# A decoder block on one core: the stage ahead of the first projection, with x's last tile shared by two engines, two rows of the sums on GpSimd, and modulation row block by row block

## The chip, the core and the metric

The kernel runs on one core of a Trainium2 chip. The engines are named as the profile names them: PE (TensorE, matmuls; PEld is its weight loads), DVE (VectorE), ACT (ScalarE), POOL (GpSimd) and SP (SyncE, which issues nearly all loads and stores). Each engine works through its own queue in order; semaphores join the queues. The metric is device time in microseconds (us) of the whole program.

## The reference, cut to what matters

One layer: a modulated RMSNorm, one input projection whose columns feed a gMLP branch and an attention branch, an output projection, a gated residual and a last RMSNorm. SEQ is 512, D_MODEL 2048, everything float32. The change touches only what comes before the input projection:

```python
cond = jax.nn.silu(c)
mod = cond @ w_ada[l] + b_ada[l]
shift, scale, gate = jnp.split(mod, 3, axis=-1)
h = rms_norm(x, norm_g[l]) * (1.0 + scale[:, None, :]) + shift[:, None, :]
z = h @ w_in[l]
```

`rms_norm` divides each row of x by the root of its mean square (plus 1e-6) and multiplies by `norm_g`. `c` has one row, so `cond @ w_ada` is a product of one vector with a 2048 x 6144 matrix.

## The kernel before

**Tiles.** x is loaded as four tiles `x0` to `x3` of 128 rows (positions) by 2048 columns, 1 MB each. The projection wants h with features on the partitions, so each normalised tile is transposed on PE in blocks of 128 x 128: `xT[kb]` holds feature block kb (0 to 15) for all 512 positions. After modulation each block is split in two, `hh` (rounded to the matmul's type) and `hl` (the rest), and each weight tile in `whi` and `wlo`; a product is hh·whi + hl·whi + hh·wlo, lines L147 to L149.

**Before the first matmul of the projection** these chains run.

1. Norm, lines L305 to L310, a loop over the four x tiles: ACT squares the tile and sums along the row (`ssq`), DVE multiplies by 1/D and adds the epsilon (L90), POOL raises the one column to the power -0.5 (L91), DVE scales the 128 x 2048 tile (L308).
2. Transposes, L318: four of them (one for each x tile) make one PSUM bank `xTp`; ACT copies the bank out to `xT` (L325). Seven banks are in use, so PE is at most seven feature blocks ahead of ACT.
3. The shift and scale of the first two feature blocks, `ada_step(0, i)` and `make_h(0)`. Shift and scale are sums over 16 row blocks ("rows" kk below) of `w_ada`, each row block weighted with a column of `sc`, which is silu(c). Row blocks come in pairs (`ada_i` holds rows 2i and 2i+1, two loads of 256 KB). Most rows are summed on DVE into `accs`, 128 x 512 in SBUF (L244 for row 0, L246 for the others). The rows in `MV = (7, 9, 11, 13, 15)` go to PE instead as matmuls that move a single column, `sc`, and add up in four columns of the PSUM bank `cb` (L239). In `make_h(0)` four matmuls with a column of ones add the 128 partitions of `accs` to the same four columns (L258); DVE forms `sh` and `gs` from them (L263 to L265); ACT makes `hh` (L269); for block 0 DVE makes `h` (L276) and `hl` (L283).
4. The first weight tiles, `raw_st`: ACT rounds them (L131, `whi`), POOL subtracts (L132, `wlo`).

After that the projection runs on PE, in stages of two feature blocks. For the next stage the same sums are made by DVE while PE works, with one difference: there the running sum `acc` lies in PSUM. `make_h(q)` then comes as a few small matmuls (`mod`) in the middle of PE's queue.

**What sets the order.** The kernel is written as a sequence, and a scheduler places each instruction in the queue of its engine by priority (`high_priority`) and by its own estimate of times; `issue_after` pins one instruction behind another. The order is fixed when the program is built. SP's loads are chained in the order of the code, and a load waits for the buffer it writes: the `ada` tiles have eight buffers, so the first pair of the next stage goes into the buffer of `ada_0`, the second into that of `ada_1`, and so on. Each load also waits for the load eight places before it. At the start PE runs 18 bf16 matmuls on a mask (`warm`, L193), whose product is not used.

Of the kernel before, what the change touches and what calls it, by code (L numbers as in the profile page):

```python
# [27 lines left out]
def trunk_kernel(  # L28
# [68 lines left out]
    WARM = 0  # L97

# [79 lines left out]
    rows = st.tile([64, P], F32, name="rows")  # L178
    for r0, nr, src in (
        (16, 32, b_ada[0, 0 : 2 * D]), (0, 16, norm_g[0]), (48, 8, ln_g[0]), (56, 8, ln_b[0]),  # L180
    ):
        nc.scalar.dma_start(rows[r0 : r0 + nr, :], src.rearrange("(a b) -> a b", b=P))
# [8 lines left out]
    def warm(lhs, rhs, n, first=False):  # L191
        for i in range(n):
            nc.tensor.matmul(  # L193
                cb[:, P : P + rhs.shape[-1]], lhs, rhs, start=first, stop=True, skip_group_check=True
            )
# [24 lines left out]
    MV = (7, 9, 11, 13, 15)  # L220

    def ada_step(q, i):
# [3 lines left out]
        for s in range(2):  # L226
            load(ga[:, :, s, :], ada_r[:, 2 * i : 2 * i + 2, s, k0 * P : k0 * P + 256])
        if i == 0:
# [3 lines left out]
        a, sb = accs[q]  # L232
        for j in range(2):
            kk = 2 * i + j
            col = sc[:, kk : kk + 1]
            if q == 0 and kk in MV:
                for s in range(2):
                    for n in range(2):
                        newest_mm[0] = nc.tensor.matmul(  # L239
                            cb[:, 2 * s + n : 2 * s + n + 1], ga[:, j, s, n * P : (n + 1) * P], col,  # L240
                            start=(kk == MV[0] and s + n == 0), stop=False, skip_group_check=True,
                        )
            elif kk == 0:
                nc.vector.tensor_scalar(a, ga[:, j], col, None, ALU.mult)  # L244
            else:
                nc.vector.scalar_tensor_tensor(  # L246
                    sb if kk == KB - 1 else a, ga[:, j], col, a, ALU.mult, ALU.add
                )
# [3 lines left out]

    def make_h(q):
        k0, nk = ADA[q]
        mp = bank("c", f"mod{q}") if q else cb
        for s in range(2):
            for j in range(nk):
                newest_mm[0] = nc.tensor.matmul(  # L258
                    mp[:, s * nk + j : s * nk + j + 1], accs[q][1][:, s, j * P : (j + 1) * P],
                    ones[:, 0:1], start=q > 0, stop=True, skip_group_check=True,  # L260
                )
        ks = slice(k0, k0 + nk)
        nc.vector.tensor_tensor(sh[:, ks], mp[:, 0:nk], bshT[:, ks], ALU.add)  # L263
        nc.vector.tensor_tensor(gs[:, ks], mp[:, nk : 2 * nk], b1[:, ks], ALU.add)
        nc.vector.tensor_tensor(gs[:, ks], gs[:, ks], ngT[:, ks], ALU.mult)  # L265
        for k in range(k0, k0 + nk):
            hh[k] = act.tile([P, S], F32R, tag="hh", name=f"hh{k}")
            hl[k] = act.tile([P, S], F32R, tag="hl", name=f"hl{k}")
            z = nc.scalar.activation(  # L269
                hh[k], xT[k], AF.Identity, bias=sh[:, k : k + 1], scale=gs[:, k : k + 1]  # L270
            )
            h = xT[k]
            if k == 0:
                first_h[0] = z
                h = st.tile([P, S], F32, name="h0", tag="acc", bufs=2)
                nc.vector.tensor_scalar(  # L276
                    h, xT[k], gs[:, k : k + 1], sh[:, k : k + 1], ALU.mult, ALU.add
                )
            else:
                nc.scalar.activation(  # L280
                    xT[k], xT[k], AF.Identity, bias=sh[:, k : k + 1], scale=gs[:, k : k + 1]
                )
            (nc.vector if k == 0 else HL).tensor_tensor(hl[k], h, hh[k].bitcast(F32), ALU.subtract)  # L283
# [18 lines left out]
    ssq = st.tile([P, NT], F32, name="ssq")  # L302
    rstd = st.tile([P, NT], F32, name="rstd")
    for t in range(NT):
# [4 lines left out]
        if t < 3:  # L309
            warm(ident, xt[t][:, 0:P], WARM)  # L310
# [843 lines left out]
```

## Time and profile before

| | us |
|---|---|
| median of 3 runs | 905.56 |
| lowest and highest of them | 905.46 and 912.02 |
| the profiled execution | 903.07 |
| its span, first to last instruction | 901.3 |
| around the span | 1.77 |

The profile is of one execution. Its chain of waits goes back from the last instruction to what released each step. A row of the timeline gives start, duration, engine, line, operation, output and inputs, shape, how many instructions are merged in it, and in brackets how long the engine was idle before it and what ended that. The duration of merged rows runs to the end of the last one. A matmul of float32 with one moving column shows as two records, so `make_h(0)`'s four matmuls are eight. Ends of matmuls are modelled; the distance between starts tells the pace.

### The profile page before, as it was taken

Reading aid. Unit: us, or ns where it says so; the run is one execution under the profiler, and the core shown is the slowest. Engines: PE = TensorE matmul, PEld = TensorE weight load, DVE = VectorE, ACT = ScalarE, POOL = GpSimd, SP = SyncE. Lnnn points to the kernel's source line nnn. Section 1 sums busy time; section 2 is a strip of 40 time slices with the busy share of each in tenths; the row PEclk is TensorE's granted clock in tenths of the full one; section 3 lists DMA queues with packets and bytes.
Section 4 is the critical chain, followed back from the end, with each engine's and each line's share of the span. In section 5 each row is a group of like instructions: output and inputs, shape, how many; then the busy total and the mean of one; then the engine's idle time right before and its main releaser. Section 6 shows DMA issues by size and latency. Waiting matters only on the chain.

```text
span 901.3 us, 12686 instructions
## 1 busy us (share of the span) xinstructions
PE 878.5 (97%) x4408; PEld 744.5 (83%) x4408; DVE 596.3 (66%) x982; ACT 444.6 (49%) x775; POOL 438.1 (49%) x338
## 2 busy tenths in 40 slices
PE   6999999999999999999999999999999999999995
PEld 4988888887888997778789888998898888888884
DVE  4768888374436866455786563456764679997687
ACT  5653332442213224465666554557465657554454
POOL 2355555425676359988998879444751000000001
PEclk7899999999999999999999999999999999999998
DMA  9999996438996164554554545677576246577575
GB/s 339 352 352 356 354 318 212 121 108 292 312 317 201 40 186 124 161 161 133 174 165 140 166 130 187 199 234 221 186 249 188 71 126 209 182 252 248 177 238 203
DMA packets 139712, 188.91 MB, mean 210 GB/s; under 512 B 9968, under 2 KB 103360, under 8 KB 139136
## 3 DMA queue, kind: packets, MB, share of 16 engines
q1 hardware_dynamic: 139216, 187.53, 65.0%
q8 instruction: 35, 0.57, 0.3%
q10 hardware_dynamic: 432, 0.57, 0.2%
q14 instruction: 29, 0.24, 0.1%
HBM read 166.90 MB, written 20.97 MB: 208 GB/s over the span
## 4 chain that ended last, share of the span: by engine, by line
PE 88%; DVE 4%; DMA 3%; issue 2%; ACT 2%; POOL 0%; SPq 0%; POOLq 0%; ACTq 0%; DVEq 0%
PE s L149 6%; PE s L147 6%; PE s L148 6%; PE vb L156 3%; PE vb L157 3%; PE vb L158 3%; PE va L158 3%; PE va L156 3%; PE va L157 3%; PE q L147 3%; PE q L149 3%; PE q L148 3%; PE gb L149 3%; PE k L149 3%; PE gb L148 3%; PE gb L147 3%
## 5 line engine op out<-in xcount | busy, mean ns | idle before, releaser
L608 POOL TENSOR_SCALAR gate<-gate,sc 128x512 f32<-128x512 f32 x60 | 106.4, 1783 | 22.6 <-DMA gate<-in_w_ada_dram 13.6
L132 POOL TENSOR_TENSOR wlo_st<-raw_st,whi_st 128x1024 fp32r<-128x1024 f32 (+3 forms) x36 | 68.4, 1905 | 51.3 <-ACT whi_st L131 48.0
L609 POOL TENSOR_TENSOR gate<-gate,gate 128x512 f32<-128x512 f32 x60 | 91.7, 1530 | 1.8
L148 PE MATMUL s<-hl,whi_st 128*128 128x512 f32 x224 | 86.8, 390 | 0.0
L147 PE MATMUL s<-hh,whi_st 128*128 128x512 f32 x224 | 86.7, 392 | 0.0
L654 POOL TENSOR_TENSOR ts<-ts 128x256 f32<-128x256 f32 x64 | 57.1, 898 | 58.2 <-DMA ts<-in_w_out_dram 55.3
L66 ACT ACTIVATE whi_p<-p 128x1024 fp32r<-128x1024 f32 x52 | 55.2, 1061 | 55.1 <-PE woZ L938 20.1
L67 DVE TENSOR_TENSOR wlo_p<-p,whi_p 128x1024 fp32r<-128x1024 f32 x52 | 63.4, 1221 | 20.2 <-ACT whi_p L66 20.1
L246 DVE SCALAR_TENSOR_TENSOR acc<-ada,sc,acc 128x512 f32<-128x512 f32 x98 | 73.9, 754 | 3.4 <-DMA ada<-in_w_ada_dram 0.5
L149 PE MATMUL s<-hh,wlo_st 128*128 128x512 f32 x224 | 76.2, 392 | 0.0
L157 PE MATMUL vb<-whi_vb,hl 128*128 128x256 f32 (+1 forms) x256 | 72.2, 285 | 0.0
L156 PE MATMUL vb<-whi_vb,hh 128*128 128x256 f32 (+1 forms) x256 | 72.0, 285 | 0.0
L158 PE MATMUL vb<-wlo_vb,hh 128*128 128x256 f32 (+1 forms) x256 | 71.3, 288 | 0.0
L981 POOL TENSOR_TENSOR sfin<-sfin,nhalf 128x1 f32<-128x1 f32 x2 | 1.5, 748 | 137.7 <-DVE sfin L1073 137.7
L131 ACT ACTIVATE whi_st<-raw_st 128x1024 fp32r<-128x1024 f32 (+3 forms) x36 | 31.3, 871 | 65.1 <-PE s L148 38.8
L147 PE MATMUL q<-hh,whi_q 128*128 128x512 f32 x128 | 50.6, 395 | 1.3 <-ACT whi_q L131 1.3
L132 DVE TENSOR_TENSOR wlo_va<-raw_va,whi_va 128x1024 fp32r<-128x1024 f32 x16 | 26.0, 1626 | 38.0 <-ACT whi_va L131 33.9
L147 PE MATMUL k<-hh,whi_k 128*128 128x512 f32 x128 | 50.2, 392 | 0.7 <-ACT whi_k L131 0.7
L147 PE MATMUL gb<-hh,whi_gb 128*128 128x512 f32 x128 | 50.4, 394 | 0.3 <-ACT whi_gb L131 0.3
L156 PE MATMUL va<-whi_va,hh 128*128 128x512 f32 x128 | 50.3, 393 | 0.0
L148 PE MATMUL q<-hl,whi_q 128*128 128x512 f32 x128 | 50.2, 392 | 0.0
L148 PE MATMUL gb<-hl,whi_gb 128*128 128x512 f32 x128 | 50.2, 392 | 0.0
(308 smaller groups left out, 2541.9 us busy)
## 6 DMA issues: line engine op xcount, KB each, us to landing
ada<-in_w_ada_dram SPq DMA_DIRECT2D x128, 256.0 KB
gate<-in_w_ada_dram SPq DMA_DIRECT2D x32, 512.0 KB
p<-ts SPq DMA_DIRECT2D x32, 512.0 KB
p<-in_w_out_dram SPq DMA_DIRECT2D x24, 512.0 KB
raw_va<-in_w_in_dram SPq DMA_DIRECT2D x16, 512.0 KB
raw_q<-in_w_in_dram SPq DMA_DIRECT2D x16, 512.0 KB
raw_k<-in_w_in_dram SPq DMA_DIRECT2D x16, 512.0 KB
raw_gb<-in_w_in_dram SPq DMA_DIRECT2D x16, 512.0 KB
```

The costliest lines, as they stand in the source:

```text
L67: return a, (eng or nc.vector).tensor_tensor(lo, src, hi.bitcast(F32), ALU.subtract)
L132: (loeng or nc.vector).tensor_tensor(lo, raw, hi.bitcast(F32), ALU.subtract)
L147: nc.tensor.matmul(pt, hi[:, j, cs], hh[k], start=(k == first), stop=False)
L148: nc.tensor.matmul(pt, hi[:, j, cs], hl[k], start=False, stop=False)
L149: nc.tensor.matmul(pt, lo[:, j, cs], hh[k], start=False, stop=(k == last))
L156: nc.tensor.matmul(o, ah[k][:, tsl], hi[:, j, :], start=(k == first), stop=False)
L157: nc.tensor.matmul(o, al[k][:, tsl], hi[:, j, :], start=False, stop=False)
L158: nc.tensor.matmul(o, ah[k][:, tsl], lo[:, j, :], start=False, stop=(k == last))
L246: nc.vector.scalar_tensor_tensor(sb if kk == KB - 1 else a, ga[:, j], col, a, ALU.mult, ALU.add)
L608: nc.gpsimd.tensor_scalar(ga[:, j], ga[:, j], sc[:, kk : kk + 1], None, ALU.mult)
L609: nc.gpsimd.tensor_tensor(a, a, ga[:, j], ALU.add)
L654: nc.gpsimd.tensor_tensor(dst, l, r, ALU.subtract)
```

## The change

- **x3.** ACT squares and sums only the first 1024 columns of `x3`; DVE does the other 1024 in one instruction (`tensor_tensor_reduce`, which starts from the epsilon term), then adds ACT's sum and divides by D. POOL's power is as before. DVE scales the first 1024 columns, ACT the other 1024.
- **Table.** A Square of one column is put on ACT between the first of its loads and the others, so ACT's table load comes there.
- **Rows.** `MV` becomes (11, 13, 15): rows 7 and 9 go to DVE. Rows 2 and 3 (`ada_1`) leave DVE: POOL multiplies each with its column of `sc` and adds the two, and DVE adds the result to `accs` in one instruction ahead of row 10. Row 14, the last on DVE, is done as two instructions, one for each feature block.
- **PE's order.** All transposes of blocks 0 to 13 come first (`HB` goes from 12 to 13), then rows 11, 13, 15, with four mask matmuls (`GAPW`) ahead of row 13 and four ahead of row 15.
- **Modulation.** `make_h(0)` takes the two feature blocks one after the other: two matmuls with ones, `sh`, `gs`, `hh` for block 0, then the same for block 1.

The core of the diff:

```diff
-    MV = (7, 9, 11, 13, 15)
+    MV = (11, 13, 15)
...
+        if q == 0 and i == 1:
+            for j in range(2):
+                nc.gpsimd.tensor_scalar(ga[:, j], ga[:, j], sc[:, 2 + j : 3 + j], None, ALU.mult)
+            nc.gpsimd.tensor_tensor(ga[:, 0], ga[:, 0], ga[:, 1], ALU.add)
+            side.append(ga)
+            return
+        if q == 0 and i == 5:
+            nc.vector.tensor_tensor(a, a, side[0][:, 0], ALU.add)
...
+                    if kk > MV[0]:
+                        warm(cmask[:, 0:P], cmask[:, 0 : S - P], GAPW, after=newest_mm[0])
...
-                nc.vector.scalar_tensor_tensor(
-                    sb if kk == KB - 1 else a, ga[:, j], col, a, ALU.mult, ALU.add
-                )
+                for c_ in ((slice(0, P), slice(P, 2 * P)) if q == 0 and kk == KB - 2 else (slice(0, 256),)):
+                    nc.vector.scalar_tensor_tensor(
+                        (sb if kk == KB - 1 else a)[:, :, c_], ga[:, j, :, c_], col, a[:, :, c_],
+                        ALU.mult, ALU.add,
+                    )
...
+            nc.scalar.activation(
+                junk[:, 0:HD], xt[t][:, 0:HD], AF.Square, accum_out=ssq[:, t : t + 1]
+            )
+            rt = rstd[:, t : t + 1]
+            nc.vector.tensor_tensor_reduce(
+                out=junk[:, HD:D], in0=xt[t][:, HD:D], in1=xt[t][:, HD:D], scale=1.0,
+                scalar=EPS * D, op0=ALU.mult, op1=ALU.add, accum_out=rt,
+            )
+            nc.vector.tensor_tensor(rt, rt, ssq[:, t : t + 1], ALU.add)
+            nc.vector.tensor_scalar(rt, rt, 1.0 / D, None, ALU.mult)
+            power = nc.gpsimd.tensor_tensor(rt, rt, nhalf[:, 0:1], ALU.pow)
+            scaled = XS.tensor_scalar(xt[t][:, 0:HD], xt[t][:, 0:HD], rt, None, ALU.mult)
+            nc.scalar.activation(xt[t][:, HD:D], xt[t][:, HD:D], AF.Copy, scale=rt)
...
+                if i < 2:
+                    es.enter_context(tc.issue_after((power if i else scaled).ins))
+                ada_sums(0, i, loaded[i])
-    HB = 12
+    HB = 13
```

In DVE's queue, around the scaling of x3 and the sums, there stood before (x_105 is x3; accs is the running sum; ada_i the pair of rows 2i and 2i+1; lines of the kernel before):

```order
L204 COPY cols<-cols_p 128x64
L212 TENSOR_SCALAR b_137<-cols 128x16
L244 TENSOR_SCALAR accs_145<-ada_0_142,sc 128x512
L90 TENSOR_SCALAR rstd<-ssq 128x1
L246 SCALAR_TENSOR_TENSOR accs_145<-ada_0_142,sc,accs_145 128x512
L308 TENSOR_SCALAR x_105<-x_105,rstd 128x2048
L246 SCALAR_TENSOR_TENSOR accs_145<-ada_1_148,sc,accs_145 128x512 x2
L246 SCALAR_TENSOR_TENSOR accs_145<-ada_2_153,sc,accs_145 128x512 x2
L246 SCALAR_TENSOR_TENSOR accs_145<-ada_3_158,sc,accs_145 128x512
```

In the changed kernel the same queue, from the scaling of x3 (now x_107, half of it) to the first `sh`, reads:

```order
L366 TENSOR_SCALAR x_107<-x_107,rstd 128x1024
L275 TENSOR_SCALAR accs_192<-ada_0_144,sc 128x512
L278 SCALAR_TENSOR_TENSOR accs_192<-ada_0_144,sc,accs_192 128x512
L278 SCALAR_TENSOR_TENSOR accs_192<-ada_2_150,sc,accs_192 128x512 x2
L278 SCALAR_TENSOR_TENSOR accs_192<-ada_3_153,sc,accs_192 128x512 x2
L278 SCALAR_TENSOR_TENSOR accs_192<-ada_4_156,sc,accs_192 128x512 x2
L256 TENSOR_TENSOR accs_192<-accs_192,ada_1_147 128x512
L278 SCALAR_TENSOR_TENSOR accs_192<-ada_5_159,sc,accs_192 128x512
L278 SCALAR_TENSOR_TENSOR accs_192<-ada_6_162,sc,accs_192 128x512
L278 SCALAR_TENSOR_TENSOR accs_192<-ada_7_165,sc,accs_192 128x2x128 x2
L319 TENSOR_TENSOR sh<-cb,cols 128x1
```

Before, two rows were summed ahead of x3's scaling and nine behind it; now all of them stand behind it: eleven rows, the last of them in two halves, and the addition of POOL's result.

POOL's queue of the changed kernel, from the powers to the first weight tile, where three instructions are new (the third and fourth row below):

```order
L91 TENSOR_TENSOR rstd<-rstd,nhalf 128x1 x3
L365 TENSOR_TENSOR rstd<-rstd,nhalf 128x1
L251 TENSOR_SCALAR ada_1_147<-ada_1_147,sc 128x512 x2
L252 TENSOR_TENSOR ada_1_147<-ada_1_147 128x512
L133 TENSOR_TENSOR wlo_st_1_0_0_377<-raw_st_1_0_0_373,whi_st_1_0_0_376 128x512
```

The two multiplications and the addition for rows 2 and 3 stand right behind x3's power, where DVE's half scaling of x3 and its sums also begin.

PE's queue of the changed kernel behind the last transpose of block 13 (cb is the bank of the sums; the first row stands between the mask matmuls, whose weight loads the order lists too):

```order
L267 MATMUL cb<-sc,ada_6_162 128x1 x4
L199 LDWEIGHTS cmask
L199 MATMUL cb<-cmask 128x384
L199 LDWEIGHTS cmask
L199 MATMUL cb<-cmask 128x384
L199 LDWEIGHTS cmask
L199 MATMUL cb<-cmask 128x384
L199 LDWEIGHTS cmask
L199 MATMUL cb<-cmask 128x384
L267 MATMUL cb<-sc,ada_7_165 128x1 x4
L312 MATMUL cb<-ones,accs_192 128x1 x4
L381 MATMUL xTp_348<-ident,x_101 128x128
```

Before, the matmuls with ones were followed by three blocks of transposes (twelve) and then the projection; now by two blocks (eight). Further on the order of every engine is what it was.

More of the change, by code (lines that the diff above doesn't have):

```diff
@@ L97, in trunk_kernel @@
     WARM = 0
+    GAPW = 4
     newest = [None]
@@ L189, in trunk_kernel, with warm @@
     cb = bank("c", "cb")
-    def warm(lhs, rhs, n, first=False):
+    def warm(lhs, rhs, n, first=False, after=None):
         for i in range(n):
-            nc.tensor.matmul(
-                cb[:, P : P + rhs.shape[-1]], lhs, rhs, start=first, stop=True, skip_group_check=True
-            )
+            with ExitStack() as es:
+                if after is not None:
+                    es.enter_context(tc.issue_after(after.ins))
+                nc.tensor.matmul(
+                    cb[:, P : P + rhs.shape[-1]], lhs, rhs, start=first, stop=True,
+                    skip_group_check=True,
+                )
     warm(cmask[:, 0:P], cmask[:, 0 : S - P], BUSY, True)
@@ L236, in ada_step, with moving @@
             if q == 0 and kk in MV:
-                for s in range(2):
+                def moving(ga=ga, j=j, kk=kk, col=col):
+                    if kk > MV[0]:
+                        warm(cmask[:, 0:P], cmask[:, 0 : S - P], GAPW, after=newest_mm[0])
                     for n in range(2):
[L239 to L242, printed above, removed]
+                        for s in range(2):
+                          with tc.issue_after((newest_mm[0] or newest_tr).ins):
+                            newest_mm[0] = nc.tensor.matmul(
+                                cb[:, 2 * s + n : 2 * s + n + 1], ga[:, j, s, n * P : (n + 1) * P],
+                                col, start=(kk == MV[0] and s + n == 0), stop=False,
+                                skip_group_check=True,
+                            )
+                later_mm.append(moving)
             elif kk == 0:
@@ L255, in make_h @@
         mp = bank("c", f"mod{q}") if q else cb
[L256 to L283, printed above, removed]
+        for z in range(nk if q == 0 else 1):
+            js = [z] if q == 0 else list(range(nk))
+            for s in range(2):
+                for j in js:
+                    newest_mm[0] = nc.tensor.matmul(
+                        mp[:, s * nk + j : s * nk + j + 1], accs[q][1][:, s, j * P : (j + 1) * P],
+                        ones[:, 0:1], start=q > 0, stop=True, skip_group_check=True,
+                    )
+            ks = slice(k0 + js[0], k0 + js[-1] + 1)
+            m0 = mp[:, js[0] : js[-1] + 1]
+            m1 = mp[:, nk + js[0] : nk + js[-1] + 1]
+            nc.vector.tensor_tensor(sh[:, ks], m0, bshT[:, ks], ALU.add)
+            nc.vector.tensor_tensor(gs[:, ks], m1, b1[:, ks], ALU.add)
+            nc.vector.tensor_tensor(gs[:, ks], gs[:, ks], ngT[:, ks], ALU.mult)
+            if q == 0:
+                modulate(k0 + z)
@@ L285, in ada_steps @@
+        if q:
+            for k in range(k0, k0 + nk):
+                modulate(k)
     def ada_steps(q):
```

54 lines of the change are left out of this document (44 added, 10 removed).

## The prediction

> **What bounds the kernel now.** I read the page's first lines, then the chain of waits over the first 60 us, then the table of stretches, then the timeline there. From the page:
>
> ```profile
> span 901.3 us, 12686 instructions
> PE 878.5 (97%) x4408; PEld 744.5 (83%) x4408; DVE 596.3 (66%) x982; ACT 444.6 (49%) x775; POOL 438.1 (49%) x338
> ```
>
> PE is busy 97% of the span, so 23 us without PE work are all there is, most of it ahead of the projection. The change can only move the projection's start; behind it PE's queue is unchanged, so a move of the start goes to the end as it is, if nothing later catches it. The chain of waits (start, length, what) there:
>
> ```profile
> 17.31 1.06 POOL rstd L91
> 18.39 1.30 DVE x L308
> 22.34 0.93 PE xTp L318 x8
> 24.94 3.54 PE cb L239 x24
> 28.48 1.71 PE cb L258 x8
> 30.18 2.66 PE xTp L318 x12
> 32.85 1.35 PE s L147 x5
> 47.36 0.79 PE mod L258 x8
> ```
>
> x3's scaling (L308) is the last thing PE waits for; from 19.7 on PE itself is the chain. The same kind of instruction has two paces: a transpose takes 0.93/8 = 0.116 us at 22.3 and 2.66/12 = 0.222 at 30.2; a record with one moving column takes 1.71/8 = 0.214 at 28.5 and 0.79/8 = 0.099 at 47.4. The table of stretches (from:to, length, busy time of PE, PEld, DVE, ACT, POOL with counts, granted clock, DMA share, GB/s) shows why:
>
> ```profile
> 16.09:19.50 3.41, 2.76 (x13) 2.35 (x12) 2.93 (x7) 0.17 (x2) 1.05 (x1) 0.50 1.10 350
> 19.50:22.92 3.42, 3.18 (x30) 3.19 (x31) 3.28 (x6) 2.82 (x6) 0.00 (x0) 1.00 1.10 349
> 22.92:26.33 3.41, 3.41 (x35) 3.41 (x32) 2.83 (x4) 3.41 (x8) 0.00 (x0) 1.00 1.11 353
> 26.33:29.74 3.41, 3.41 (x18) 3.41 (x17) 0.75 (x1) 1.29 (x3) 1.94 (x2) 0.50 1.08 346
> 29.74:33.15 3.41, 3.41 (x17) 3.31 (x17) 2.90 (x8) 2.41 (x5) 0.27 (x1) 0.50 1.10 351
> 33.15:36.56 3.41, 3.41 (x17) 2.80 (x16) 3.27 (x5) 1.90 (x4) 1.30 (x1) 1.00 1.10 353
> ```
>
> The granted clock halves at 26.33, behind a stretch of mostly single-column records, and comes back at 33.15, behind one full of transposes. Before, the projection runs at half clock until 33.15; its start counts as 32.9 at full pace (it begins at about 32.65, as the twelve transposes end, and loses half of 0.5 us).
>
> DVE does not bind before: its sums end at 27.10 and then it waits 3.12 us for PE. These rows carry the terms below:
>
> ```profile
> 14.56 0.55 POOL L91 TENSOR_TENSOR rstd<-rstd,nhalf 128x1 f32<-128x1 f32 x1 [1.46 <-DVE rstd L90]
> 17.31 1.05 POOL L91 TENSOR_TENSOR rstd<-rstd,nhalf 128x1 f32<-128x1 f32 x1 [2.20 <-DVE rstd L90]
> 14.25 1.91 ACT L306 ACTIVATE junk<-x 128x2048 bf16<-128x2048 f32 x1 [0.20 <-DMA x<-in_x_dram]
> 15.14 1.29 DVE L308 TENSOR_SCALAR x<-x,rstd 128x2048 f32<-128x2048 f32 x1 [0.67 <-POOL rstd L91]
> 16.68 0.48 DVE L244 TENSOR_SCALAR accs<-ada,sc 128x512 f32<-128x512 f32 x1
> 17.20 0.75 DVE L246 SCALAR_TENSOR_TENSOR accs<-ada,sc,accs 128x512 f32<-128x512 f32 x1
> 19.60 6.26 DVE L246 SCALAR_TENSOR_TENSOR accs<-ada,sc,accs 128x512 f32<-128x512 f32 x8
> 26.35 0.75 DVE L246 SCALAR_TENSOR_TENSOR accs<-ada,sc,accs 128x512 f32<-128x512 f32 x1 [0.50 <-DMA ada<-in_w_ada_dram]
> 30.22 0.16 DVE L263 TENSOR_TENSOR sh<-cb,cols 128x2 f32<-128x2 f32 x1 [3.12 <-PE cb L258]
> 30.57 0.75 DVE L244 TENSOR_SCALAR acc<-ada,sc 128x512 f32<-128x512 f32 x1
> 30.74 1.52 ACT L269 ACTIVATE hh<-xT,sh,gs 128x512 fp32r<-128x512 f32 x2 [2.60 <-DVE gs L265]
> ```
>
> **The change, part by part.**
>
> *x3 and the table load.* x3 lands at 14.25 (ACT waited for it), and the table load ahead of x0 is no longer the first thing ACT does with x, so only x0 to x2 can be earlier. Four 1 MB tiles arrive evenly, x2 some 2.5 us ahead of x3, at 11.7; its square (1.91) and sum, DVE's small step, POOL's power (0.55) bring DVE to x2's scaling at about 14.7, done at 16.0 (before: 16.43). Only then does DVE's queue reach its half of x3's squares. No such row exists; the custom DVE reduction of 128x512 costs:
>
> ```profile
> L491 DVE CUSTOM_DVE_ANT_0 s<-s,cmask 128x512 f32<-128x512 f32 x16 | 11.4, 714 | 3.0 <-PE s L490 3.0
> ```
>
> so 1024 columns cost 0.7 to 1.4, taken 1.3 (double, less one start), to 17.3. Reading the sum, the copy of `cols` and three small steps, 0.1 to 0.2 each: 17.9. Power 0.55: 18.5. Before, it ended at 18.36. So sharing x3 gives nothing up to the factor. Half the scaling lies between 0.48 (512 columns) and 1.29 (2048), 0.75: 19.25 in place of 19.68, 0.4 us won for PE.
>
> *PE.* 35 transposes are left then (7 + 28), 24 single-column records and eight mask matmuls. By the paces above the first two take 4.1 + 2.4 us all at full clock, 7.8 + 5.1 at half. The mask matmuls:
>
> ```profile
> 1.52 5.21 PE L193 MATMUL cb<-cmask 128*128 128x384 bf16 x18 [1.52 <-POOL cmask L74]
> ```
>
> 0.29 each, 2.3 for eight, half of that were those all at half clock. PE is through at 27.1 (row 15 lands at 26.35, by DVE's wait, and costs 0.8) to 34.5; with the clock back after one busy stretch, as at 19.50, about 30. The 16 records less are worth 1.6 to 3.4 us, but only if PE is still last.
>
> *DVE becomes last.* Behind 18.5 it has the half scaling 0.75, row 0 0.45, seven rows at 6.26/8 = 0.78 (5.5), the addition 0.72, two rows 1.56, and the first half of row 14, between 0.38 and 0.75, 0.45: 9.4 us, to 27.9, the second half to 28.35. Rows 7 and 9, moved from PE, take the place of 2 and 3, and the two that stood ahead of x3's scaling come behind it. That is already 0.8 later than 27.10, and POOL's work is not in it yet.
>
> *Two rows on POOL.* Their price is in the gate stage:
>
> ```profile
> L608 POOL TENSOR_SCALAR gate<-gate,sc x60: 1559/1568/2637, 329.4 to 560.0; 128x512 f32<-128x512 f32 x60
> L609 POOL TENSOR_TENSOR gate<-gate,gate x60: 1275/1292/3976, 331.0 to 562.9; 128x512 f32<-128x512 f32 x60
> ```
>
> 2 x 1.57 + 1.28 = 4.4 us, from 18.5 to 22.9, ahead of DVE's addition at about 25. It looks hidden. But minimum and maximum lie far apart, and a pair of rows shows what stretches them:
>
> ```profile
> 217.43 1.28 POOL L633 TENSOR_TENSOR tsptl<-tsptl 128x512 f32<-128x512 f32 x1
> 217.46 2.33 DVE L132 TENSOR_TENSOR wlo_va<-raw_va,whi_va 128x1024 fp32r<-128x1024 f32 x1 [2.50 <-ACT whi_va L131]
> L67 DVE TENSOR_TENSOR wlo_p<-p,whi_p 128x1024 fp32r<-128x1024 f32 x52 | 63.4, 1221 | 20.2 <-ACT whi_p L66 20.1
> ```
>
> The same DVE form takes 1.22 alone and 2.33 when it starts 0.03 behind a POOL instruction: it waits it out, less 0.14 us of start. POOL waits likewise: x3's power took 1.05, not 0.55, beside row 1 on DVE (17.20 to 17.95). `accs` and `ada` are both in SBUF, as in these pairs. So each of POOL's three instructions stops DVE for its length: 4.4 - 3 x 0.14 = 4.0 us. The bounds are 0 (they fall into DVE's own waits, of which it has none here) and 4.4. I take 4.0: first half at 31.9, second at 32.35.
>
> The Trainium skill, "SBUF — State Buffer", section "Who interferes with whom", says a DVE instruction with two SBUF inputs contends with a GpSimd instruction that reads SBUF, and whichever is first holds the shared pair for its whole instruction. By that the term is the full 4.4 us and the sum 0.4 later.
>
> *Row block by row block.* Block 0 needs two matmuls with ones (four records): 0.86 at half clock. Half clock, because PE waits from about 30 to 31.9 behind single-column records, as at 26.33. Then `sh` and `gs` 0.45, `hh` 0.8: 31.9 + 0.86 + 0.1 + 0.45 + 0.05 + 0.8 = 34.15. PE meanwhile does block 1's four records to 33.65 and eight transposes at 0.213 to 35.35, and starts there. `hl` (h 0.54, three small steps 0.42, `acc` 0.75, `hl` 0.69 behind 33.3) is there at 35.7, before the sixth matmul. The clock is back after a stretch of transposes, at 36.56 if the boundaries stay; 1.2 us at half pace cost 0.6.
>
> *Loads.* The second pair of the next stage goes into `ada_1`'s buffer, now free only after DVE's addition, 18.5 + 0.75 + 0.45 + 5.5 + 0.72 + 4.0 = 29.9; all later loads queue behind it on SP.
>
> ```profile
> 24.82 1.07 SPq L107 DMA_DIRECT2D ada<-in_w_ada_dram  x2
> 43.67 0.75 DVE L246 SCALAR_TENSOR_TENSOR accs<-ada,sc,acc 128x512 f32<-128x512 f32 x1
> ```
>
> They are 5.1 us late. Their sums ended at 44.42 for a consumer at 47.36, 2.9 of slack, and PE is 3 later itself: hidden, barely.
>
> *Sum.* Start at full pace 35.35 + 0.6 = 35.95 against 32.9: +3.05 us, on 903.07 (span 901.3) 906.1. The median of the runs shown, 905.56, is 2.5 above the profiled execution. Clock boundaries need not fall alike in each execution, and a start that waits for DVE depends less on them, so I don't add the 2.5 in full: 906.6.
>
> **Rivals.**
>
> *POOL doesn't stop DVE: faster.* One mechanism: the three instructions run beside the sums. First half at 27.9; with the clock held, ones 0.4, `sh` and `gs` 0.5, `hh` 0.8: 29.6, 0.35 for `hl`, so 29.95 and -2.95, which the 2.9 of slack at 47.36 also allows: 900.2; with the clock lost 902.1. It decides where DVE is held up by less than 4.0 - 3.05 = 1.0 us. For it: the one overlapping row of this very form, at 17.20, was not itself stretched. Against it: there POOL came second, and paid.
>
> *The clock stays up.* The eight mask matmuls are there between the single-column rows. Then ones 0.4, block 0's `hh` at 33.7, the transposes done with it, and `hl` (35.25) holds the sixth matmul up by 0.35: 34.1, +1.2, 904.3. Against it: 22.92 to 26.33 held more transposes than the mask matmuls amount to, and the next stretch was at 0.50.
>
> The skill's "TensorE: Matmul & The Clock Gate", Part 1, has the clock fall after an idle stretch of 3.4 us. PE would hardly be idle so long; by that rule this rival holds, with its 904.3. The row at 22.92 speaks against it: PE listed busy for all 3.41 us, and the next at 0.50.
>
> *One more stretch at half clock, or the late loads show.* 3.4 us at half pace are +1.7: 907.8; PE through only at 34.5 gives 906.1 + 2.6 = 908.7; loads not hidden by PE's own delay, 5.1 - 2.9 more: 908.3.
>
> *No difference:* the terms cancel, within 0.5 of 903.07 to 905.56.
>
> **How the numbers follow.** Forecast 0.50 (905.5 to 907.2); clock stays up 0.13; faster rival 0.22 (900.2 to 902.1 on the profiled execution, up to 904.6 by the runs); slower rivals 0.10; no difference 0.05. Range 902.6 to 909.0: it leaves out the faster rival's lower half and the longest tail. A measurement of this kernel tells a change from none at about 1%, 9 us; no case here moves so far, so within 1% is 0.96, faster 0.01, slower 0.03 (a lot of runs like the 912.02).
>
> **What would show it.** Right: DVE's sums end near 32 with rows of 2 us among them, POOL's L251 rows above 1.57, PE idle before the matmuls with ones, the projection at 35 to 36. Wrong: ten rows at 0.75 beside POOL's (faster rival); granted clock 1.00 from 26 to 36; PE waiting at `mod` near 50 (loads).

## The result, and the profile after

| | before | after |
|---|---|---|
| median of 22 runs each, same chip, us | 904.88 | 911.53 |
| lowest and highest | 902.58, 912.02 | 907.30, 915.78 |
| ratio to before, 95% interval | | 1.0057, 1.0041 to 1.0073 |
| profiled execution, its span | 903.07, 901.3 | 911.00, 908.9 |

The changed kernel is slower by 6.65 us, where 906.6 was predicted (902.6 to 909.0). In a second comparison on another occasion (below) it was 1.0045, 1.0019 to 1.0070, that is 4.8 us. The two profiled executions lie 7.6 us apart.

The page's first lines of the changed kernel say as little as those of before: PE still 97% busy.

```profile
span 908.9 us, 12686 instructions
PE 880.3 (97%) x4400; PEld 744.0 (82%) x4400; DVE 604.7 (67%) x990; ACT 445.6 (49%) x777; POOL 441.0 (49%) x341
```

The table of stretches of the changed kernel, cut at its clock's own boundaries (from:to, length, busy time of PE, PEld, DVE, ACT, POOL, granted clock, DMA share, GB/s):

```profile
21.72:25.13 3.41, 3.41 (x32) 3.30 (x32) 3.30 (x4) 3.41 (x9) 0.65 (x1) 1.00 1.11 347
25.13:28.54 3.41, 2.75 (x24) 2.38 (x21) 3.21 (x5) 2.07 (x5) 1.43 (x1) 1.00 1.09 352
28.54:31.96 3.42, 1.15 (x5) 1.06 (x5) 2.64 (x6) 0.00 (x0) 1.63 (x2) 0.50 1.10 347
31.96:35.37 3.41, 3.41 (x15) 3.22 (x16) 2.98 (x9) 2.80 (x5) 0.00 (x0) 0.50 1.09 352
35.37:38.78 3.41, 3.41 (x10) 2.64 (x9) 3.27 (x5) 0.51 (x2) 1.28 (x1) 0.50 1.09 360
38.78:42.20 3.42, 3.42 (x17) 2.81 (x16) 3.28 (x5) 1.16 (x2) 1.59 (x2) 1.00 0.60 186
```

Three stretches at half clock stand here, 28.54 to 38.78, where before had two, 26.33 to 33.15; PE is idle for two thirds of the first of them. Its timeline, and DVE's and POOL's, say what it waited for:

```profile
17.44 1.18 DVE L366 TENSOR_SCALAR x<-x,rstd 128x1024 f32<-128x1024 f32 x1 [0.66 <-POOL rstd L365]
17.39 3.40 POOL L251 TENSOR_SCALAR ada<-ada,sc 128x512 f32<-128x512 f32 x2
18.54 0.82 DVE L275 TENSOR_SCALAR accs<-ada,sc 128x512 f32<-128x512 f32 x1
19.40 6.67 DVE L278 SCALAR_TENSOR_TENSOR accs<-ada,sc,accs 128x512 f32<-128x512 f32 x7
20.88 1.50 POOL L252 TENSOR_TENSOR ada<-ada 128x512 f32<-128x512 f32 x1
26.89 3.95 DVE L278 SCALAR_TENSOR_TENSOR accs<-ada,sc,accs 128x512 f32<-128x512 f32 x4
27.11 3.06 POOL L133 TENSOR_TENSOR wlo_st<-raw_st,whi_st 128x512 fp32r<-128x512 f32 x2 [4.74 <-ACT whi_st L132]
30.50 1.01 PE L312 MATMUL cb<-ones,accs 128*128 128x1 f32 x4 [2.62 <-DVE accs L278]
31.83 1.01 PE L312 MATMUL cb<-ones,accs 128*128 128x1 f32 x4 [0.31 <-DVE gs L320]
34.30 2.06 PE L148 MATMUL s<-hh,whi_st 128*128 128x512 f32 x4
```

PE is through with its rows at 27.9 and waits 2.62 us for DVE. DVE's sums end at 30.84. They were held up twice: by POOL's two products and sum, and once more by POOL's first weight split (L133), which starts at 27.11 and did not meet the sums before, since they ended at 27.10. The projection begins at 34.30 and runs at half pace to 38.78.

The last row of each kernel that a later comparison needs is the first matmul of `q`, far behind the change:

```profile
334.97 0.40 PE L147 MATMUL q<-hh,whi_q 128*128 128x512 f32 x1
338.20 0.40 PE L148 MATMUL q<-hh,whi_q 128*128 128x512 f32 x1
```

So the start accounts for 3.2 of the 7.6 us of this pair. The other 4.4 arise behind 338 us, among instructions that stand in the same order as before.

### The profile page after: what moved, and what is told of

Read it like the earlier page. It is cut to its first block, busy times and chain, and to the rows that moved or that the text cites. A ratio compares the mean times of both kernels' runs of the same rounds, so it can differ in the third digit from the quotient of the medians.

```text
span 908.9 us, 12686 instructions
## 1 busy us (share of the span) xinstructions
PE 880.3 (97%) x4400; PEld 744.0 (82%) x4400; DVE 604.7 (67%) x990; ACT 445.6 (49%) x777; POOL 441.0 (49%) x341
## 4 chain that ended last, share of the span: by engine, by line
PE 76%; DMA 8%; DVE 6%; POOL 4%; issue 3%; ACT 2%; SPq 1%; POOLq 0%; DVEq 0%; ACTq 0%
PE s L148 6%; PE s L150 6%; PE s L149 6%; PE va L159 3%; PE va L157 3%; PE va L158 3%; PE q L148 3%; PE q L149 3%; PE vb L157 3%; PE q L150 3%; PE vb L158 3%; PE vb L159 3%; PE gb L150 2%; PE gb L149 2%; PE gb L148 2%
## 5 line engine op out<-in xcount | busy, mean ns | idle before, releaser
L673 POOL TENSOR_SCALAR gate<-gate,sc 128x512 f32<-128x512 f32 x60 | 103.1, 1729 | 26.6 <-DMA gate<-in_w_ada_dram 16.0
L133 POOL TENSOR_TENSOR wlo_st<-raw_st,whi_st 128x1024 fp32r<-128x1024 f32 (+3 forms) x36 | 69.2, 1927 | 48.4 <-ACT whi_st L132 46.1
L133 DVE TENSOR_TENSOR wlo_va<-raw_va,whi_va 128x1024 fp32r<-128x1024 f32 x16 | 25.2, 1573 | 39.1 <-ACT whi_va L132 34.9
```

The source lines that it names most:

```text
L133: (loeng or nc.vector).tensor_tensor(lo, raw, hi.bitcast(F32), ALU.subtract)
L673: nc.gpsimd.tensor_scalar(ga[:, j], ga[:, j], sc[:, kk : kk + 1], None, ALU.mult)
```

## The experiments

Names that begin with b or before are the kernel before with an edit, those with a or after the changed kernel with one. Each comparison has its own runs of before, on the same chip. "First q" is the start of the row just shown, in each profile.

### Is the start all there is?

b_late11 puts eleven mask matmuls ahead of the matmuls with ones in the kernel before, to delay its start:

```diff
         if kb == HB:
             with tc.high_priority(offset=200):
+                for i in range(11):
+                    with tc.issue_after(newest_mm[0].ins):
+                        nc.tensor.matmul(cb[:, P : P + S - P], cmask[:, 0:P], cmask[:, 0 : S - P], ...)
                 make_h(0)
```

> The kernel before with eleven more mask matmuls ahead of the matmuls with ones, nothing else added. At 0.29 us each they put the projection's start off by about 3.1 us, the size of the shift that the change shows at 52 us (51.92 against 48.33). Theory 'pure shift': a start that is later by 3.1 us moves the end by 3.1 us, so about 908.0 against 904.9 before, ratio 1.0034. Rival 'it grows': a later start meets loads and splits behind 340 us at a worse moment and costs about twice itself, as in the profiles of before and after (3.6 us at 52 us, 7.6 us at the end): 911 to 912, ratio 1.007. Second rival, the masks bring the clock back a stretch sooner and the shift is smaller than 2 us: below 907.

Measured 907.39 against 905.70, ratio 1.0018 (0.9987 to 1.0048), span 904.3. The start did not come later but earlier, which is the second rival's mechanism (its time, below 907, was missed by 0.4): the clock stays at 1.00, the eleven masks take 0.18 us each, and the single-column records and transposes behind them run at twice the pace that they had at 28.5 to 32.8 before.

```profile
26.46 1.95 PE L331 MATMUL cb<-cmask 128*128 128x384 bf16 x11
28.25 0.95 PE L258 MATMUL cb<-ones,accs 128*128 128x1 f32 x8
29.06 1.51 PE L318 MATMUL xTp<-ident,x 128*128 128x128 f32 x12
30.61 1.68 PE L147 MATMUL s<-hh,whi_st 128*128 128x512 f32 x5
```

First q at 333.58, 1.4 ahead of before, and yet the span is 3 us longer. So the stretch from first q to the end isn't a constant. Four more profiles, of the two kernels unchanged, say how far it varies:

> The kernel before, unchanged, in a second profiled execution. What is read is the stretch from the first q matmul to the end, 566.3 us in the first profile (334.97 to 901.3), against 570.7 in the changed kernel's. Theory 'the end varies': the changed kernel, and the four kernels run so far (568.4 to 572.8 with starts at or ahead of that of before), show no price of a late start but the spread of executions; a second execution of before then has 567 to 572. Rival 'the late part is the change's': 566 to 567 again.

> The kernel before, unchanged, in a third profiled execution; the same expectation as for the second. It also shows how far the moment at which x3's scaling begins (18.39 in the first profile, 17.36 to 17.47 in the changed kernel and in before with masks) varies between executions, and which stretches have half the clock.

> The changed kernel, unchanged, in a second profiled execution. Theory 'the end varies': the first q matmul again at 337.5 to 339.5, 2.5 to 4.5 later than in before, and the stretch from there to the end anywhere from 567 to 573. Rival 'the late part is the change's': 570.5 or more in both executions. A third possibility, the start itself varies with the phase of the clock's stretches: the first q matmul 1.7 or 3.4 us off 338.2.

> The changed kernel, unchanged, in a third profiled execution; the same expectation as for the second.

The spans were 909.8 and 909.2 for before, 908.9 and 908.7 for the changed kernel. before_2 ran at half clock from 10.38 to 41.10, so its first q is at 341.86; before_3 starts as the first profile did, 335.02, and loses its time later: 574.2 us from there to the end against 566.3. Part of that loss is two stretches at half clock far behind the change, at 699.12 and here (granted clock third from the end):

```profile
432.88:436.29 3.41, 3.41 (x12) 2.93 (x11) 2.80 (x7) 1.33 (x2) 3.41 (x2) 0.50 0.60 179
```

Eight of the 18 profiles taken have one or two such stretches between 407 and 703 us, in both kernels; the first profile of before, on which the prediction stands, has none, and the shortest way from first q to the end of all 18 (table below). The rival's 566 to 567 for before falls with 567.9 and 574.2. The changed kernel's first q is at 338.20, 337.39 and 336.67, and its stretch in the two new executions is 571.5 and 572.0: inside the theory's 567 to 573, but also above the rival's 570.5, so these profiles don't decide whether part of its late loss is the change's.

b_late60 has sixty masks in the same place:

> The kernel before with sixty mask matmuls ahead of the matmuls with ones in place of eleven. At the 0.18 us that the eleven took (1.95 for eleven, at full clock) the start is 49 x 0.178 = 8.7 us later than with eleven, so the first q matmul at about 342.3 (333.6 there, 335.0 before). Theory 'a shift goes to the end as it is': the stretch from there to the end is 567 to 573 again and the median 8.7 above that of eleven (907.4), about 916, between 914 and 918. Rival 'a late start grows': as in the pair of profiles, where 3.2 us at the first q matmul had become 7.6 at the end, it costs about twice itself, 922 or more, with 575 us or more from the first q matmul to the end.

Measured 918.09 against 906.04, 1.0146 (1.0100 to 1.0192; six runs). Its profile has first q at 341.75 and 569.7 us behind it, as the theory says; but that is the fastest of its runs (913.12). In the others the granted clock of the whole run is lower (0.979 to 0.988 against 0.993). Where they lost it no profile shows, so the median tells nothing on the size of a pure shift.

### What holds the start up?

```diff
# a_dve_rows: rows 2 and 3 on DVE again
-        if q == 0 and i == 1:
...
-            return
-        if q == 0 and i == 5:
-            nc.vector.tensor_tensor(a, a, side[0][:, 0], ALU.add)
# a_split_waits: ahead of POOL's first weight split
+            held_split.append(nc.gpsimd.tensor_copy(ssq[:, 0:1], accs[0][1][:, 1, 255:256]))
# a_hold: behind row 15
             for f in later_mm:
                 f()
+            warm(cmask[:, 0:P], cmask[:, 0 : S - P], 16, after=newest_mm[0])
```

> The changed kernel with rows 2 and 3 summed on DVE again; POOL's two products, its sum and DVE's addition are gone. Theory 'POOL stops DVE': without them DVE does one row more (twelve full rows and the addition become thirteen rows), 0.75 us, but loses the 2 us that the products held it up, and it ends before POOL's first weight split begins at 27.1: sums done at 27.7 to 28.6 in place of 30.84, matmuls with ones at about 28.5, start 2.3 to 3 us earlier, 907.3 to 909.2. Rival 'the rows themselves': DVE is held up by its own number of rows, the sums still end at 30 to 31 and the time stays at 911 to 912.

> The changed kernel in which POOL's first weight split waits for the last row of DVE's sums (POOL copies one column of the sums ahead of it). Theory 'the split stops DVE': rows 12 and 14 took 1.63 and 1.10 us beside the two splits in place of 0.75 and 0.38, so the sums end 1.6 us earlier, at about 29.3, and the start with them: about 910, or 908 if a half-clock stretch goes as well. The splits are then done at 29.4 + 1.2 + 0.9 = 31.5, before the projection needs them at 35. Rival 'the loss only moves': the splits then hold up sh, gs, h or hl for the same 1.6 us, start as before, 911 to 912.

> The changed kernel with sixteen more mask matmuls on PE behind row 15, where it waited 2.6 us for DVE. Theory 'the idle stretch costs the clock': with PE streaming from 27.9 to 30.5 the granted clock stays at 1.00 through 28.5 to 38.8, the records with ones take 0.1 us and the projection starts at about 33 at full pace in place of 36.4: 908 to 909. Rival 'the single-column records cost it': the stretch from 28.5 still shows 0.50, the masks take 0.29 us each and end at 32.5, the start is 1 to 2 us later: 912.5 to 914.

Against 905.70 for before: 907.99 (1.0025, 0.9998 to 1.0053), 908.02 (1.0008, 0.9982 to 1.0035) and 907.42 (1.0011, 0.9986 to 1.0036). Each alone brings first q back to that of before: 334.72, 335.07, 334.95. DVE's rows in a_dve_rows, then in a_split_waits:

```profile
17.44 0.75 DVE L358 TENSOR_SCALAR x<-x,rstd 128x1024 f32<-128x1024 f32 x1 [0.66 <-POOL rstd L357]
18.11 0.48 DVE L267 TENSOR_SCALAR accs<-ada,sc 128x512 f32<-128x512 f32 x1
18.62 11.16 DVE L270 SCALAR_TENSOR_TENSOR accs<-ada,sc,accs 128x512 f32<-128x512 f32 x13
```

```profile
26.81 2.46 DVE L284 SCALAR_TENSOR_TENSOR accs<-ada,sc,accs 128x512 f32<-128x512 f32 x4
30.01 0.82 DVE L327 TENSOR_TENSOR gs<-gs,cols 128x1 f32<-128x1 f32 x1
30.94 1.12 DVE L302 TENSOR_SCALAR h<-xT,gs,sh 128x512 f32<-128x512 f32 x1
```

Without POOL's products the half scaling takes 0.75 in place of 1.18 and row 0 0.48 in place of 0.82; the sums end at 29.8, later than the 27.7 to 28.6 expected, since the split still meets the last of them. Without the split beside them the last four instructions take 2.46 in place of 3.95. So the rival "the rows themselves" falls, and so does "the loss only moves", though a part does move: `gs` takes 0.82 for 0.16, `h` 1.12 for 0.55. In a_hold DVE's sums end as late as in the changed kernel, at 30.74; for the start only the clock differs (table of stretches):

```profile
25.50:28.90 3.40, 3.40 (x26) 2.42 (x25) 3.24 (x4) 1.49 (x3) 1.88 (x2) 1.00 1.09 353
28.90:32.30 3.40, 2.18 (x17) 1.65 (x16) 2.88 (x10) 0.74 (x1) 1.17 (x1) 1.00 1.10 350
32.30:35.70 3.40, 3.40 (x20) 2.87 (x18) 3.33 (x6) 2.56 (x5) 0.67 (x1) 1.00 1.02 338
```

With the masks the clock stays at 1.00 to 897 us and the projection starts at 32.62 at full pace. (The masks also move something behind first q, as the last part of this section shows, so a_hold's time is not that of the start alone.) a_three has all three edits (with six masks), and b_mix tries to hold the clock in the kernel before with real work, each row on PE between two blocks of transposes:

```diff
-    HB = 12
+    HB = 14
...
+        if 10 <= kb <= 14:
+            with tc.high_priority(offset=200):
+                moving_rows.pop(0)()
```

> The changed kernel with three edits together: rows 2 and 3 on DVE again, POOL's first weight split behind the last row, six mask matmuls behind row 15. Each took 3 us off the start alone. Theory 'three separate holds on one chain': DVE's thirteen rows take 13 x 0.75 with nothing beside them and end at 28.4 (29.7 with rows on DVE alone, 30.84 in the changed kernel), the clock stays at 1.00, and the projection starts at 30.5 to 31.2, 1.4 to 2 us ahead of the mask version's 32.6: first q matmul at 333 to 333.6, median 1.5 to 2 below the mask version's 907.4, about 905.5 to 906, or 0.998 to 1.000 of before in this comparison. Rival 'one hold stands for all': once the clock is held the rest is hidden, start 32 to 32.6, 907 to 908.

> The kernel before with the rows on PE set between the transposes: row 7 behind block 10, then one row behind each of blocks 11 to 14, the matmuls with ones, and four transposes left. No masks, nothing moved to other engines. Theory 'the clock falls where single-column records come in a bunch': with 16 transposes spread among them the stretches stay at 1.00, PE is through at about 27.5 to 28, and the projection starts at 29.5 to 30.5 at full pace, 2 us ahead of before (32.0 to 32.9): first q matmul at about 333, median 1.5 to 2.5 below before, ratio 0.997 to 0.9985. Rival 'spread or not, they count as idle': half clock from 26 to 33 as before, start and time as before within 1 us.

> The changed kernel, unchanged, timed on the same chip as the other three of this call, and a fourth profile of it. Expected from its first measurement (ratio 1.0057) 1.004 to 1.007 of before, first q matmul at 336.5 to 338.5, and from there to the end 570 to 573.

In one comparison with before at 906.04: a_three 906.47 (1.0000, 0.9976 to 1.0023), b_mix 908.54 (1.0026, 0.9997 to 1.0054), the changed kernel unchanged (after_4) 910.81 (1.0045, 1.0019 to 1.0070), its first q at 338.10. In a_three the thirteen rows take 9.54 with nothing beside them, and the start is at 30.68, as expected; but the clock falls from 30.90 to 34.31, and PE waits 1.36 us at 53.88 for a rounding on ACT (under "A better version"), so first q is at 335.91 and not 333. The theory of b_mix falls:

```profile
24.65:28.06 3.41, 3.41 (x34) 3.41 (x33) 1.25 (x2) 2.54 (x6) 0.00 (x0) 1.00 1.09 353
28.06:31.47 3.41, 2.29 (x11) 1.89 (x11) 1.90 (x5) 1.41 (x4) 2.22 (x2) 0.50 1.07 345
```

A stretch with transposes among the single-column records, PE listed busy throughout, is followed by half clock all the same.

### What lengthens the end?

Read behind first q, PE's starts in all 18 profiles agree to 0.15 us up to one load. SP issues it 30.46 us after first q (30.58 in b_late11): 512 KB of `gate` for POOL. It lands 34.2 to 34.4 after first q in eleven profiles and 34.7 to 36.1 in seven. What differs is when a packet of the DMA queue that the profile calls "instruction" runs (16 KB, 0.9 to 2.1 us on its DMA engine). From the trace, the last two columns behind first q (after_pad, before_pad, before_fewer and a_four come further down):

| kernel | first q | span | first q to end | packet | load lands |
|---|---|---|---|---|---|
| before | 334.97 | 901.3 | 566.3 | 30.65 | 34.33 |
| before_2 | 341.86 | 909.8 | 567.9 | 30.20 | 34.28 |
| before_3 | 335.02 | 909.2 | 574.2 | 30.15 | 34.29 |
| b_late11 | 333.58 | 904.3 | 570.7 | 24.41 | 34.40 |
| b_mix | 335.32 | 904.3 | 569.0 | 30.67 | 34.29 |
| a_hold | 334.95 | 903.3 | 568.4 | 23.82 | 34.39 |
| a_three | 335.91 | 902.6 | 566.7 | 30.22 | 34.27 |
| b_late60 | 341.75 | 911.4 | 569.7 | 43.09 | 34.25 |
| a_four | 334.93 | 905.1 | 570.2 | 30.30 | 34.25 |
| after_pad | 338.03 | 909.0 | 571.0 | 30.10 | 34.26 |
| before_pad | 333.82 | 901.7 | 567.9 | 24.29 | 34.17 |
| after | 338.20 | 908.9 | 570.7 | 31.49 | 34.81 |
| after_2 | 337.39 | 908.9 | 571.5 | 32.66 | 35.86 |
| after_3 | 336.67 | 908.7 | 572.0 | 32.53 | 35.83 |
| after_4 | 338.10 | 910.9 | 572.8 | 31.43 | 34.67 |
| a_dve_rows | 334.72 | 905.4 | 570.7 | 31.52 | 35.90 |
| a_split_waits | 335.07 | 907.9 | 572.8 | 32.42 | 35.62 |
| before_fewer | 341.44 | 910.7 | 569.3 | 32.88 | 36.10 |

The late group has nothing to do with a late start: a_dve_rows and a_split_waits start with before. It goes by how many instructions PE has ahead of that place, which moves where its blocks of instructions are fetched. Matmuls and weight loads ahead of first q, counted in the trace: 3238 to 3240 in the seven with the late load; 3250 to 3253 in the seven with the packet at 30.1 to 30.7; 3265 to 3275 in the three with it at 23.8 to 24.4; 3372 in b_late60. The load's landing is counted in sixteen updates of a semaphore: in all 18 profiles fifteen of them have come by 34.4, and only the last one is late in the seven. Two kernels raise the number of instructions by twelve and leave every other one where it was, a third lowers it by about as many in the kernel before:

```diff
# after_pad, before_pad: behind the first 18 masks
+    warm(cmask[:, 0:P], cmask[:, 0:1], 6, True)
# before_fewer: in place of the first 18 masks
+    for i in range(BUSY - 6):
+        nc.tensor.matmul(cb, cmask[:, 0:P], cmask[:, 0:S], start=True, stop=True, skip_group_check=True)
```

> The changed kernel with six more mask matmuls of one column right behind the first eighteen, where PE waits for x0 anyway: twelve PE instructions more ahead of everything, all else in the same order. Theory 'where the instruction packets fall': the packet that ran 31.4 to 32.7 us behind the first q matmul now runs at about 30.2, as in the kernel with three edits, which has the same count; the gate load issued at 30.46 lands at 34.3 in place of 34.7 to 35.9, PE waits under 1.2 us at the gb weights of 404 in place of 0.9 to 2.5, and the time falls by 2 to 3 us with the start unchanged (first q matmul 336.7 to 338.2): ratio to before 1.002 to 1.0035. Rival 'it is the start': nothing moves, 1.0045 to 1.0057 as before.

> The kernel before with the same six mask matmuls of one column: it then has the changed kernel's count of PE instructions. Theory 'where the instruction packets fall': the packet moves from 30.2 to 30.7 behind the first q matmul to 31.4 to 32.7, the gate load lands at 34.7 to 35.9, and the time rises by 2 to 3 us with the start unchanged (first q matmul near 335.0): ratio to before 1.002 to 1.0035. Rival 'it is the start': 1.000.

> The kernel before with twelve mask matmuls of 512 columns at its beginning in place of eighteen of 384: twelve PE instructions fewer ahead of everything, about the same PE time (6144 columns for 6912), all else in the same order. Theory 'where the instruction packets fall': the packet that ran 30.2 to 30.7 us behind the first q matmul now runs at 31.4 to 32.7, the gate load issued at 30.46 lands at 34.7 to 35.9 in place of 34.3, POOL waits about 3 us for it in place of 1.4, and the time rises by 1 to 3 us with the first q matmul at 333.5 to 335: ratio to before 1.001 to 1.0035. Rival 'only the start counts': load and later stage as in before, ratio 0.999 to 1.001.

The packet among the DMA queues (count, MB, share of 16 engines in windows of 1.6, 3.0, 1.6 and 2.0 us), then POOL's wait for the load: in the kernel before the packet runs ahead of the load's data, in after_2 amid it, in after_pad ahead again, in before_fewer amid it.

```profile
q8 instruction: 1, 0.02, 3.7%
369.55 3.11 POOL L608 TENSOR_SCALAR gate<-gate,sc 128x512 f32<-128x512 f32 x2 [1.45 <-DMA gate<-in_w_ada_dram]
```

```profile
q8 instruction: 1, 0.02, 1.9%
373.50 3.11 POOL L673 TENSOR_SCALAR gate<-gate,sc 128x512 f32<-128x512 f32 x2 [2.98 <-DMA gate<-in_w_ada_dram]
```

```profile
q8 instruction: 1, 0.02, 4.1%
372.53 3.11 POOL L674 TENSOR_SCALAR gate<-gate,sc 128x512 f32<-128x512 f32 x2 [1.37 <-DMA gate<-in_w_ada_dram]
```

```profile
q8 instruction: 1, 0.02, 2.9%
377.80 3.11 POOL L609 TENSOR_SCALAR gate<-gate,sc 128x512 f32<-128x512 f32 x2 [3.21 <-DMA gate<-in_w_ada_dram]
```

In after_pad the packet is at 30.10, the load lands at 34.26, and the time is 909.81 against 906.87, 1.0017 (0.9986 to 1.0048): the size expected, with an interval that reaches both theories; its profile takes 571.0 us from first q to the end, no less than the changed kernel's 570.7. In before_fewer the packet is at 32.88, the load lands at 36.10, and the time is 907.74 against 904.88, 1.0032 (1.0007 to 1.0058): 2.9 us slower than before, with the late load. Its profile is of an execution at half clock to 40.65, so its first q, 341.44, is not that of most of its runs, and whether its other masks moved the start as well isn't known. before_pad missed its purpose: the packet went to 24.29 (the two kernels' counts of PE instructions were not alike after all), the load lands at 34.17, and the time stays, 906.66, 1.0004 (0.9971 to 1.0037).

How the late load reaches PE: SP's later loads stand behind loads of `gate` that wait for POOL to free their buffer. In the chain of waits, first of before, then of after_2:

```profile
395.48 4.84 DMA raw_gb<-in_w_in_dram
400.40 1.06 ACT whi_gb L131
```

```profile
397.33 1.61 POOL gate L674
398.94 6.57 DMA raw_gb<-in_w_in_dram
405.60 1.06 ACT whi_gb L132
```

Behind first q, that load starts at 60.5 in before and 61.6 in after_2 and takes 1.7 us longer, for a reason that isn't shown, and PE (timeline, before and then after_2) waits for it 2.08 us in place of 0.28:

```profile
401.51 0.50 PE L147 MATMUL gb<-hh,whi_gb 128*128 128x512 f32 x1 [0.28 <-ACT whi_gb L131]
```

```profile
406.70 0.50 PE L148 MATMUL gb<-hh,whi_gb 128*128 128x512 f32 x1 [2.08 <-ACT whi_gb L132]
```

How much PE loses by it can be read directly: the 2800 matmuls behind first q come in the same order in all 18 profiles, so the start of each can be set against the earliest of the 18 (from the trace, us behind first q):

| matmul | load on time, eleven: range, mean | load late, seven: range, mean |
|---|---|---|
| a `gb` behind the wait, 73 | 0.00 to 0.47, 0.2 | 0.85 to 4.31, 2.3 |
| a later `gb`, 351 | 0.00 to 4.03, 1.9 | 0.71 to 4.61, 2.2 |
| the last, 556 | 0.00 to 7.77, 2.9 | 2.93 to 6.48, 5.0 |

So the stage itself loses, and with the start of before too (a_dve_rows 2.00, a_split_waits 2.79). In after_2 and after_3 a stretch at half clock follows the wait (from 408.51 and from 407.55), which makes theirs the largest, 4.31 and 4.07. But 351 us behind first q other waits have all but closed the gap, and most of what opens it again lies near 700 us, far from this load. That the stage's loss is the loss at the end is therefore not shown. For before_fewer the stage shows 0.95 us of the 2.9.

### A better version

a_four is a_three with the split behind block 0's `h` in place of the sums, and four of the last transposes between the matmuls with ones of the two blocks.

> The kernel with three edits and two more: POOL's first weight split waits for block 0's h in place of the sums (it had stretched gs to 1.01 and h to 1.12 us), and four of the eight last transposes stand between the matmuls with ones of block 0 and those of block 1. Theory: hh of block 0 is done at 29.8 in place of 30.6 and the last transposes at 30.2, so the projection starts at 30.0 to 30.4, and with transposes in the wait the clock stays at 1.00: first q matmul at 333 to 334 against 335.0 before; time 1 to 2 us below before, ratio 0.998 to 0.999. Rival 'the clock falls all the same': first q matmul 335 to 336 and a ratio of 1.000.

Measured 906.01 against 906.87, ratio 0.9983 (0.9955 to 1.0010), first q at 334.93: the lowest median of its comparison, not shown to be faster than before. `gs` and `h` take 0.16 and 0.55 again and the clock stays at 1.00 through the start at 30.71, but x3's scaling began 0.5 us later in this execution than in a_three's, and first q missed the 333 to 334 expected. An earlier start is caught further on:

```profile
52.94 0.50 PE L153 MATMUL s<-hh,whi_st 128*128 128x512 f32 x1 [1.37 <-ACT whi_st L132]
```

ACT makes both `xT` of the second stage's blocks here before it rounds these weights, as in a_three; in the kernel before it rounds weights between the two, and PE doesn't wait there.

## Why the prediction was wrong

**The start: right in size, in part by luck.** Predicted 3.05 us later. First q came at 338.20, 337.39, 336.67 and 338.10, 337.6 on average, against 335.0 in two of three profiles of before: 2.6 us. That the start counts is shown by the edits that take it back: each alone brings the ratio from 1.0045 to 1.0057 down to between 1.0008 and 1.0025, no longer clear of 1. Two of them keep the late load, and the interval of one, a_split_waits (up to 1.0035), lies below the first measurement's (from 1.0041).

**Its parts.** x3's scaling began at 17.44, 17.95, 17.94 and 18.11 in the four profiles, not at 18.5 (x2's scaling began at 13.89 in the first, not at 14.7); in before it was 18.31 to 18.39, so this edit won about 0.2 to 0.9. Most signs set for "right" came, about 1 us earlier than stated: DVE's sums end at 30.84 with stretched rows, of which the longest took 1.65 us and not 2, PE is idle ahead of the matmuls with ones, POOL's products take 1.70 each, the projection begins at 34.30. But the term "POOL stops DVE by 4.0 us" was too large. The half scaling lost 0.43, row 0 0.34, the next seven instructions 6.67 - 7 x 0.78 = 1.2: 2.0 us for three POOL instructions of 4.9. By the Trainium skill, "SBUF — State Buffer", section "Who interferes with whom", whichever comes first holds the pair for its whole instruction; here the stop was less than half of the three instructions' time. What the prediction missed beside it is the split at 27.11, 1.5 us, a row of POOL that sums ending at 27.10 had never met. The two errors cancel in part, and that is luck: from the scaling's start to the end of the sums 13.4 us, predicted 13.85.

The clock was to be back at 36.56 and to cost 0.6; it came back at 38.78 and cost half of 34.30 to 38.78, 2.2 us, in the first profile, and at 36.46, 35.49 and 37.83 in the others. The matmuls with ones of block 1 wait for DVE's `gs` of block 0 (31.83), which the prediction had them not do.

**The loads ahead of the second stage: hidden, as predicted.** The next stage's sums ended at 46.30, its `mod` matmuls ran at 50.79 without a wait.

**The step that failed: "a move of the start goes to the end as it is, if nothing later catches it".** The 906.6 lies 4.9 us below the first measurement: 1.3 by its base (next paragraph), -0.45 by the start (2.6 for 3.05), and 4.05 behind first q, where the prediction put nothing. In the second comparison the three are 2.5, -0.45 and 2.2. PE's queue behind the start is the same, but its place among the packets of the instruction queue isn't. Shown are the load's delay in seven of seven profiles with the packet at 31.4 to 32.9 and in none of the others, that twelve PE instructions move it both ways, and that PE loses 0.85 to 4.31 us in the gate stage with it, at most 0.47 without, whatever the start. How much of this is left at the end stays open: 2.9 us by before_fewer (0.6 to 5.2, its start not known), 2.5 to 3.6 by after_pad against the changed kernel's two comparisons (intervals overlap), 2.1 in the mean of first q to end (571.4 in the seven profiles, 569.3 in the other eleven), where the eleven alone spread over 7.9.

**The sum was also made on the wrong base.** The profiled 903.07 lies 1.8 below the median of 22 runs, and its end (566.3) is the shortest of 18; only 0.5 of the 2.5 us seen then was added. With before_fewer's 2.9 for the load, taken as it is: 904.88 + 2.6 + 2.9 = 910.4, against 911.53; in the second comparison 906.04 + 5.5 = 911.5, against 910.81.

**The rivals.** "POOL doesn't stop DVE" fell: it did by 3.5 us in all, above the 1.0 that decided. "The clock stays up" is what a_hold does with sixteen masks more; with the change's eight it didn't. "One more stretch at half clock" came true in part, at 1.6 us (2.2 less the 0.6 counted) for the 1.7 given; its late loads stayed hidden. "No difference" fell with an interval that begins at 1.0041.

**Open.** Why a packet of 0.9 to 2.1 us among the load's data delays its landing by 0.4 to 1.8 us (one part in sixteen is late, but the trace doesn't name its DMA engine); and the rest of the spread of 566 to 574 us behind first q, in which PE waits for weights and `q` loads near 430, 612 and 697 us by another amount in each execution and in which the half-clock stretches lie.

## What to carry to other kernels

Before adding a change's gain or loss to a profiled execution, find out where that execution lies among the runs, and add the rest of the way to the median. When work is moved to another engine or made later, list what the other engines start in the new interval: a neighbour that was always a moment too late to collide (POOL's split, 0.7 us behind the last sum) now collides. A wait on PE ahead of dense work can cost the clock as well as its length; sixteen matmuls on a mask in that wait were worth as much here as removing the wait's cause. And an unchanged queue behind a change is not an unchanged time: compare the two traces there, from a common instruction on, in more than one execution of each.

## What the runs showed of the hardware

- Fetching instructions is traffic on the core's 16 DMA engines, as data is: 35 packets of 16 KB in the queue "q8 instruction". One of them amid a load of 512 KB goes with a landing 0.4 to 1.8 us later, and twelve instructions of PE more or fewer decide whether it does. In the one comparison clear of 1 (before_fewer) the kernel's time went up by 0.32% (0.07 to 0.58) with it. The Trainium skill, "Runtime: NRT & Kernel Launch", section "Instruction fetch mechanics", has the blocks of 16 KiB, which agrees, and calls the cost of crossing one mostly hidden, which these runs don't bear out where a load waited for is in flight: POOL waited 2.98 us in place of 1.45.
- A stretch in which the profile lists PE busy for all of 3.41 us can be followed by half clock when much of it is records with one moving column (b_mix, 24.65 to 28.06), while one with PE busy for only 2.18 of 3.40 us, at the end of sixteen bf16 masks of 384 columns, was followed by full clock (a_hold, 28.90 to 32.30).
- A DVE instruction beside POOL was stretched also where it has one tensor input: the half scaling 1.18 for 0.75, row 0 0.82 for 0.48, `h` 1.12 for 0.55. `gs`, with two inputs of one column, took 0.82 for 0.16.
